# A hybrid mixer layer: order of the opening's weight casts, statistics and scale products

## The chip, the cores and the metric

The kernel runs on one core of a Trainium2 chip. The metric is the device time in microseconds (us) of one execution; lower is better. Engines are named as in the profile: PE is TensorE (matrix products and transposes), DVE is VectorE, ACT is ScalarE, POOL is GpSimd, SP is SyncE, whose queue issues nearly all DMAs.

## The reference

One layer with S = 2048 rows and D = 1024 columns, fp32. A modulated layer norm of x is projected, goes through a gated linear recurrence and an attention with forget gates, is projected back and normed again. Only the first lines matter for the opening:

```python
c_act = jax.nn.silu(c)
mod = c_act @ w_ada[l] + b_ada[l]
shift, scale, gate = jnp.split(mod, 3, axis=-1)
h = _layer_norm(x) * (1.0 + scale) + shift
proj = h @ w_in[l]
xr, zr, q, k, v, za, fl = jnp.split(proj, split_idx, axis=-1)
xc = _causal_depthwise_conv(xr, conv_w[l], conv_b[l])
y_r = _rms_norm(_rg_lru(xc, ...)) * silu(zr)
y_a = _rms_norm(_forgetting_attention(q, k, v, log_f)) * silu(za)
y = jnp.concatenate([y_r, y_a], axis=-1) @ w_out[l]
x = _layer_norm(ALPHA * x + gate * y) * ln_gain[l] + ln_bias[l]
```

## The kernel before

The rows are cut into four chunks (0 to 3) of 512 rows, each of four tiles of 128 rows. The columns D are cut into eight slabs k of 128. The opening, up to about 160 us, computes h transposed and the projection xr = h @ w_in[:, 0:512] of all four chunks; later stages project v, k, z, q and run the recurrence, the attention and the output.

**Norm of a tile** (`norm_tile`, L270, with `ln_stats`, L241). VectorE takes statistics (L244, L246) and adds eps (L248); GpSimd raises to the power -1/2 (rs, L250); VectorE makes nm = -mean x rs (L252); ScalarE applies both to one half of the tile or to both (L274), GpSimd to the other (L276).

**Column scale.** The factor 1 + scale of slab k needs a column block of w_ada (tile `wadab`, L640). TensorE multiplies the eight or four 128-row blocks of it with silu(c) (tile `psc`); from slab 2 on VectorE first folds the other half into a partial sum `sub` (L646, L648). VectorE writes the result into `Acol` (L653).

**First pass, chunks 0 and 1.** The products are fp32r with both operands in a high and a low half. For each slab, `load_w32` (L657) loads a row block of w_in (`wrow`), ScalarE casts it to the high half (L661) and GpSimd subtracts for the low half (L663). `make_h32` (L380) transposes the four normed tiles on TensorE (`ptr`, L387), ScalarE scales to the high half (L388), VectorE makes the low half (L389); for chunk 0 GpSimd joins both again (L378) into a spare part of XL. `xr32` (L610) does the twelve products of a slab: high by high, low weight by high, high weight by low. `xr32_out` copies the four sums to XL (L619). VectorE also takes column maxima of the weights (L167, `xam`) for the fp16 scales of the later chunks.

**Shift.** c_act @ w_ada for the shift (L745 to L753): slabs 0 to 4 are multiplied by ScalarE (L231) and added by GpSimd (L234), slabs 5 to 7 go through VectorE (L225, L227). VectorE adds the two parts (L811) ahead of the products `pada` (L824). `make_scale` (L337) turns the scale and the shift into Ash and Bcol.

**Second pass, chunks 2 and 3.** fp16 in two halves: `make_hk` (L394) transposes, ScalarE scales (hf, L400) and casts the high half (hT, L354), VectorE makes the low half (L355); `xr_k` does twelve products per slab. `finish_h` does the same for chunks 0 and 1 from the joined h. The maxima of the V weights (`amn`, L717 through L167) are taken in this pass.

**What sets the order.** The code is written in the order wanted; a scheduler with a timeline model then fixes each engine's queue. `tc.issue_after(ins)` holds back an instruction until the named one. Each engine runs its queue in order. SP's DMAs wait for their buffers and for the DMA issued eight places earlier. `spin` issues products of zeros on TensorE (22 + 12 + 8 of them in the opening). `QB` (L904) holds four query buffers of the attention; GpSimd clears one row of each (L1302).

Of the kernel before, what the change touches and what calls it, by code (L numbers as in the profile page):

```python
# [38 lines left out]
def hybrid_mixer(  # L39
# [201 lines left out]
    def ln_stats(halves, eps):  # L241
        st = sm([P, 2, 6], "bst")
        for g in range(2):
            nc.vector.bn_stats(st[:, g, :], halves[g])  # L244
# [3 lines left out]
        last["ve"] = nc.vector.tensor_scalar(ve, mv[:, 1:2], eps, None, ALU.add).ins  # L248
# [1 line left out]
        last["pow"] = nc.gpsimd.tensor_tensor(out=rs, in0=ve, in1=mhalf[:, 0:1], op=ALU.pow).ins  # L250
# [1 line left out]
        nc.vector.scalar_tensor_tensor(nm, mv[:, 0:1], -1.0, rs, ALU.mult, ALU.mult)  # L252
# [17 lines left out]
    def norm_tile(hv, n):  # L270
        rs, nm = ln_stats(hv, EPS)
        for g in range(2):
            if g < n:
                nc.scalar.activation(hv[g], hv[g], AF.Identity, scale=rs, bias=nm)  # L274
            else:
                last["pow"] = nc.gpsimd.tensor_scalar(hv[g], hv[g], rs, nm, ALU.mult, ALU.add).ins  # L276
# [103 lines left out]
    def make_h32(ci, k, xs):  # L380
        if k % 2 == 0:
            h32[ci, k // 2] = sb.tile([P, 2, 2, CH], F32R, name="h32", tag="H", bufs=8)
        t = h32[ci, k // 2]
        ps = bank("C", "ptr")
        ks = slice((k % 4) * P, (k % 4 + 1) * P)
        for i in range(4):
            nc.tensor.transpose(ps[:, i * P:(i + 1) * P], xs[i][k // 4][:, ks], ident)  # L387
# [269 lines left out]
    def load_w32(k):  # L657
# [3 lines left out]
        nc.scalar.copy(w[:, 0], raw)  # L661
# [138 lines left out]
    for k in range(KT + 2):  # L800
# [11 lines left out]
        if k > 1:  # L812
            xr32(pss, 1, k - 2)
        tick()
        if 3 <= k < 3 + 4:
            with tc.issue_after(last["lo"]), tc.issue_after(hi_act[1, k]):
                wu.append((split_T(xraw[k - 3], xrec[:, k - 3:k - 2]), xun[:, k - 3:k - 2]))
# [31 lines left out]
    new_h(2)  # L849
    new_h(0)  # L850
    for k in range(KT + 1):
        if k < KT:
            make_hk(2, k, xs2)
        if k > 0:
            xr_k(2, k - 1)
        if k < KT:
            with tc.issue_after(hi_act[2, k]),tc.issue_after(last["pow2"]):
                finish_h(0, k)
# [819 lines left out]
```

## Time and profile before

| | us |
|---|---|
| median of 3 runs (lowest, highest) | 1141.88 (1139.88, 1142.59) |
| profiled execution | 1142.41 |
| its span | 1140.7 |
| TensorE busy | 1091.2 (96%) |
| VectorE, ScalarE, GpSimd busy | 784.1, 708.3, 625.5 |
| first product of chunk 0, 1 and 2 in the opening | 20.44, 58.73, 93.79 |

In a timeline each line is a start, a duration, the engine, the line of the code, the operation, the tile written and the tiles read, the count of merged instructions and, in brackets, the idle time ahead with what ended it. An engine that waits costs time only if the end of the program hangs on it. The granted clock is the share of full speed that TensorE was given.

### The profile page before, as it was taken

How to read it: one execution, taken by the hardware profiler on the slowest of the kernel's cores; microseconds unless marked ns; L12 is line 12 of the kernel's file. 1: busy time of each engine (PE TensorE's matmuls, PEld its weight loads, DVE VectorE, ACT ScalarE, POOL GpSimd, SP SyncE). 2: the span in 40 equal slices, each digit the busy share in tenths (PEclk: the TensorE clock that was granted, in tenths of full speed). 3: DMA queues.
4: the chain of work that ended last, by engine and by line, in shares of the span. 5: the costliest groups of instructions: out<-in, count | busy, mean ns of one | idle time of the engine just before them, and what ended most of it. 6: DMA issues, size and time to landing. Idle time of an engine off the chain costs nothing.

```text
span 1140.7 us, 20267 instructions
## 1 busy us (share of the span) xinstructions
PE 1091.2 (96%) x7473; PEld 612.0 (54%) x7473; DVE 784.1 (69%) x1449; ACT 708.3 (62%) x1242; POOL 625.5 (55%) x655
## 2 busy tenths in 40 slices
PE   9999999999999999999889899999999999999887
PEld 6775545454544444444455455656555565566544
DVE  7877577776777963486655456678777877787546
ACT  3547746664767511544576677879777887787820
POOL 5725533454455300743267746878777687777731
PEclk8898999999999999999999999999999999999999
DMA  8862057210224711764454445124423134310111
GB/s 287 245 192 90 1 147 214 75 56 20 56 56 120 228 69 49 251 192 136 130 153 116 132 117 156 52 80 117 131 87 121 54 122 121 100 56 22 45 47 55
DMA packets 109415, 128.36 MB, mean 113 GB/s; under 512 B 10316, under 2 KB 79540, under 8 KB 109316
## 3 DMA queue, kind: packets, MB, share of 16 engines
q1 hardware_dynamic: 109088, 127.01, 36.6%
q8 instruction: 58, 0.95, 0.4%
q14 instruction: 41, 0.34, 0.1%
q10 hardware_dynamic: 228, 0.06, 0.0%
HBM read 97.57 MB, written 29.46 MB: 111 GB/s over the span
## 4 chain that ended last, share of the span: by engine, by line
PE 67%; DVE 10%; ACT 9%; issue 6%; POOL 4%; DMA 2%; SPq 1%; DVEq 0%; ACTq 0%; POOLq 0%
PE pj L93 26%; PE pout L93 13%; PE pst L93 8%; PE acc L93 6%; PE pmx L93 5%; PE pq L93 5%; ACT pf L1343 2%; DVE mc L1315 1%; PE pgate L93 1%; ACT ph L1345 1%; DVE wadab L648 1%; POOL XL L636 1%; POOL ph L1347 1%; DVE xres L1442 1%; ACT L515 1%
## 5 line engine op out<-in xcount | busy, mean ns | idle before, releaser
L1347 POOL TENSOR_TENSOR ph<-pf,ph 128x512 f16<-128x512 f32 (+2 forms) x240 | 266.6, 1125 | 110.9 <-ACT ph L1345 102.1
L93 PE MATMUL pj<-hT,wT 128*128 128x512 f16 x1440 | 321.8, 381 | 4.3 <-DVE sza L1192 2.6
L93 PEld LDWEIGHTS <-wT 128*128 128x128 f16 x1792 | 168.8, 98 | 199.9 <-issue 12.2
L1343 ACT ACTIVATE pf<-pst,bias 128x512 f32<-128x512 f32 (+1 forms) x320 | 196.7, 632 | 82.8 <-PE pst L93 80.5
L1315 DVE TENSOR_REDUCE mc<-pmx 128x1 f32<-128x512 f32 (+2 forms) x320 | 183.7, 602 | 87.5 <-PE pmx L93 83.5
L1345 ACT CAST ph<-pf 128x512 f16<-128x512 f32 (+1 forms) x320 | 173.1, 567 | 11.1 <-issue 3.8
L93 PE MATMUL acc<-V,ph 128*128 128x129 f16 (+1 forms) x2176 | 158.7, 209 | 10.5 <-POOL ph L1347 5.9
L93 PEld LDWEIGHTS <-ph 128*128 128x128 f16 x2176 | 126.5, 99 | 67.9 <-POOL ph L1347 10.6
L93 PE MATMUL pst<-qs,kk 128*128 128x512 f16 (+1 forms) x320 | 112.8, 354 | 2.7 <-ACT pf L1343 1.4
L93 PE MATMUL pst<-qb,kk 65*128 65x512 f16 (+1 forms) x320 | 111.0, 355 | 0.0
L93 PE MATMUL pmx<-kk,qb 67*128 67x512 f16 (+2 forms) x320 | 105.1, 357 | 5.3 <-DVE mc L1315 2.2
L93 PE MATMUL pout<-wo,yT 128*128 128x512 f16 (+1 forms) x396 | 97.3, 377 | 1.5 <-ACT yT L1423 1.5
L93 PE MATMUL pout<-wo,yr 128*128 128x512 f16 (+1 forms) x396 | 91.0, 373 | 0.1
L93 PE MATMUL pj<-wN,hT 128*128 128x512 f16 x384 | 89.4, 378 | 0.2 <-ACT XL L846 0.2
L1349 DVE TENSOR_TENSOR ph<-pf,ph 128x512 f16<-128x512 f32 (+1 forms) x80 | 58.9, 736 | 26.4 <-ACT ph L1345 22.4
L1246 POOL TENSOR_TENSOR XL<-XL,szr 128x512 f32<-128x512 f32 x16 | 24.8, 1551 | 89.8 <-ACT szr L1243 89.8
L93 PEld LDWEIGHTS <-kk 65*128 65x128 f16 (+1 forms) x640 | 54.5, 99 | 31.3 <-issue 7.6
L93 PEld LDWEIGHTS <-hT 128*128 128x128 f16 x640 | 44.6, 96 | 48.5 <-issue 3.3
L93 PE MATMUL pq<-hT,wT 128*128 128x512 f16 x288 | 67.9, 383 | 0.2 <-DVE qhl L916 0.2
L93 PEld LDWEIGHTS <-yT 128*128 128x128 f16 x396 | 37.5, 98 | 39.1 <-ACT yT L1423 1.7
L93 PEld LDWEIGHTS <-yr 128*128 128x128 f16 x396 | 37.4, 98 | 38.1 <-issue 0.7
L491 POOL TENSOR_TENSOR xl<-xc,xh 128x512 fp32r<-128x512 f32 x16 | 22.9, 1432 | 57.1 <-ACT xh L489 55.7
(311 smaller groups left out, 1784.9 us busy)
## 6 DMA issues: line engine op xcount, KB each, us to landing
wraw<-in_w_in_dram SPq DMA_DIRECT2D x40, 512.0 KB
woraw<-in_w_out_dram SPq DMA_DIRECT2D x16, 512.0 KB
xres<-in_x_dram SPq DMA_DIRECT2D x16, 512.0 KB
out_dram<-xres SPq DMA_DIRECT2D x15, 512.0 KB
xt<-in_x_dram SPq DMA_DIRECT2D x16, 256.0 KB
wadab<-in_w_ada_dram SPq DMA_DIRECT2D x8, 512.0 KB
xt<-in_x_dram SPq DMA_DIRECT2D x8, 512.0 KB
wsh<-in_w_ada_dram SPq DMA_DIRECT2D x16, 256.0 KB
```

Source lines behind the costliest of these rows:

```text
L93: m = nc.tensor.matmul(o, lhsT=l, rhs=r, start=st, stop=sp, skip_group_check=chk)
L491: nc.gpsimd.tensor_tensor(out=xl, in0=xc, in1=xh, op=ALU.subtract)
L515: nc.scalar.activation(a, r, AF.Exp, scale=L8n[:, j:j + 1])
L636: nc.gpsimd.tensor_scalar(XL[j][:, sl], XL[j][:, sl], 1.0, cs[j], ALU.mult, ALU.add)
L648: nc.vector.scalar_tensor_tensor(sub, blk[:, q - 1], cact[:, q - 1:q], sub, ALU.mult, ALU.add)
L1246: nc.gpsimd.tensor_tensor(out=XL[j][:, sl], in0=XL[j][:, sl], in1=sz, op=ALU.mult)
L1315: nc.vector.tensor_reduce(out=mc[:, i, b:b + 1], in_=ps[:, 0:w], axis=AX.X, op=ALU.max)
L1343: nc.scalar.activation(pf32[:, 0:w], ps[:, 0:w], AF.Exp, scale=DH ** -0.5, bias=bias[:, ci, h, kt:kt + 1])
L1345: nc.scalar.copy(ph[:, 0, 0:w], pf32[:, 0:w])
L1347: nc.gpsimd.tensor_tensor(out=ph[:, 1, 0:w], in0=pf32[:, 0:w], in1=ph[:, 0, 0:w], op=ALU.subtract)
L1349: nc.vector.tensor_tensor(ph[:, 1, 0:w], pf32[:, 0:w], ph[:, 0, 0:w], ALU.subtract)
L1442: nc.vector.scalar_tensor_tensor(xt[:, ns], xt[:, ns], rs, late["lnb"][:, ns], ALU.mult, ALU.add)
```

## The change

1. **nm on GpSimd.** `ln_stats` has a flag `pool`. With it VectorE writes ng = -mean and GpSimd multiplies nm = ng x rs. Chunks 0, 2 and 3 use it; chunk 1 keeps nm on VectorE.
2. **Pins.** The weight casts of the first pass are issued behind the last ScalarE norm of chunk 0. The norms of chunk 1 are issued behind the last low half of chunk 0 at their step, one step earlier than before (k = 4 to 7).
3. **First slabs.** The transposes of a slab come ahead of its scale products (`tr_h32`, `out_h32` split `make_h32`); the twelve products of slab 0 come ahead of the scale products of slab 1. The maxima of the weights run one slab later. The spins are 12 + 32 + 1.
4. **Shift.** The first part is written into two tiles `qa0`, `qa1` of their own; slab 5's product moves to ScalarE. `QB` now lies in `qa0`, `qa1`, so its clearing waits for the shift.
5. **Chunk 2.** x of chunk 2 is loaded at k = 2 instead of 3, its norms run at k = 3 to 6 instead of 4 to 7, and its first two slabs are transposed and scaled inside the loop of chunk 1. A doubled allocation of four banks goes.
6. **V weights.** Their loads are issued behind the last raw weight load.

The core of the diff:

```diff
-    def ln_stats(halves, eps):
+    def ln_stats(halves, eps, pool):
...
-        nc.vector.scalar_tensor_tensor(nm, mv[:, 0:1], -1.0, rs, ALU.mult, ALU.mult)
+        if pool:
+            ng = sm([P, 1], "ng")
+            nc.vector.tensor_scalar(ng, mv[:, 0:1], -1.0, None, ALU.mult)
+            last["pow"] = nc.gpsimd.tensor_tensor(out=nm, in0=ng, in1=rs, op=ALU.mult).ins
+        else:
+            nc.vector.scalar_tensor_tensor(nm, mv[:, 0:1], -1.0, rs, ALU.mult, ALU.mult)
...
-        nc.scalar.copy(w[:, 0], raw)
+        with tc.issue_after(last["nact0"]):
+            nc.scalar.copy(w[:, 0], raw)
...
-                    pa[g] = ada_add_pool(pa[g], w, k)
+                    if k == 0:
+                        pa[g] = con.tile([P, CH], F32, name=f"pa{g}", tag=f"qa{g}")
+                        nc.scalar.activation(pa[g], w, AF.Copy, scale=cact[:, 0:1])
+                    else:
+                        ada_add_pool(pa[g], w, k)
+            elif k == 5:
+                with tc.issue_after(after):
+                    nc.scalar.activation(w, w, AF.Copy, scale=cact[:, k:k + 1])
+                va[g] = w
...
-    spin(22)
+    spin(32)
...
     for k in range(KT + 1):
         if k < KT:
+            with tc.issue_after(last["pe"]):
+                ps = tr_h32(0, k, xs)
+            if k == 1:
+                spin(1)
+                x32_mm(0)
             with tc.issue_after(last["x0"]), tc.issue_after(last["pe"]):
                 scale_col(k)
                 load_w32(k)
-            with tc.issue_after(last["pe"]):
-                make_h32(0, k, xs)
-            if k < 2:
-                spin(4)
+            out_h32(0, k, ps)
...
-        if 5 <= k < 5 + 4:
-            norm_tile(xs1[k - 5], 1)
+        if 4 <= k < 8:
+            with tc.issue_after(last["lo"]):
+                norm_tile(xs1[k - 4], 1, False)
...
-    pss = [bank(t, "pj") for t in "BBAA"]
     pss = [bank(t, "pj") for t in "BBAA"]
...
+        if k == 2:
+            xs2 = load_x(2)
+        if 3 <= k < 7:
+            norm_tile(xs2[k - 3], 1)
...
+        if k >= KT:
+            if k == KT:
+                flush()
+                new_h(2)
+                new_h(0)
+            make_hk(2, k - KT, xs2)
...
-            vraw = vf_load()
+            with tc.issue_after(last["raw"]):
+                vraw = vf_load()
...
-    QB = [cst([67, CH], f"qb{i}", F16) for i in range(4)]
+    qa = [con.tile([67, 2, CH], F16, name=f"qa{g}", tag=f"qa{g}") for g in range(2)]
+    QB = [qa[i // 2][:, i % 2, :] for i in range(4)]
```

GpSimd's queue around the rs of chunk 1's fourth tile, before. `w` is the low half of a weight slab, `XL<-h` the join of a slab of chunk 0, `wsh` (later `pa`) an addition of the shift, `xt` the second half of a tile of chunk 1; the second `rs` is that of the fourth tile:

```order
L250 TENSOR_TENSOR rs<-ve,mhalf 128x1
L663 TENSOR_TENSOR w_570<-wrow,w_570 128x512
L378 TENSOR_TENSOR XL_125<-h_408 128x512
L276 TENSOR_SCALAR xt<-xt,rs,nm 128x512
L234 TENSOR_TENSOR wsh<-wsh 128x512
L250 TENSOR_TENSOR rs<-ve,mhalf 128x1
L234 TENSOR_TENSOR wsh<-wsh 128x512 x2
L378 TENSOR_TENSOR XL_125<-h_408 128x512
```

The same queue now; the last `rs` but one is that of chunk 1's fourth tile, the last that of chunk 2's first:

```order
L234 TENSOR_TENSOR pa_619<-pa_619,wsh 128x512
L382 TENSOR_TENSOR XL_126<-h_548 128x512
L234 TENSOR_TENSOR pa_623<-pa_623,wsh 128x512
L281 TENSOR_SCALAR xt<-xt,rs,nm 128x512
L250 TENSOR_TENSOR rs<-ve,mhalf 128x1
L281 TENSOR_SCALAR xt<-xt,rs,nm 128x512
L250 TENSOR_TENSOR rs<-ve,mhalf 128x1
```

The fourth rs moved from ahead of slab 5's join to behind slab 7's join and the last addition.

ScalarE's queue where chunk 0 ends (the copies of the four sums to XL) and chunk 1 begins (`h_686`, its first slabs), before:

```order
L274 ACTIVATE xt<-xt,nm,rs 128x512
L388 ACTIVATE h_520<-ptr,Acol 128x512
L231 ACTIVATE wsh<-wsh,cact 128x512 x2
L388 ACTIVATE h_520<-ptr,Acol 128x512
L231 ACTIVATE wsh<-wsh,cact 128x512 x2
L388 ACTIVATE h_686<-ptr,Acol 128x512
L619 COPY XL_123<-pj 128x512
```

The same place now, with `h_700` for chunk 1:

```order
L398 ACTIVATE h_548<-ptr,Acol 128x512
L231 ACTIVATE wsh<-wsh,cact 128x512 x2
L279 ACTIVATE xt<-xt,nm,rs 128x512
L629 COPY XL_123<-pj 128x512
L629 COPY XL_124<-pj 128x512
L629 COPY XL_125<-pj 128x512
L629 COPY XL_126<-pj 128x512
L279 ACTIVATE xt<-xt,nm,rs 128x512
L398 ACTIVATE h_700<-ptr,Acol 128x512
```

The norm of the fourth tile and the first scaling of chunk 1 moved behind the four copies.

VectorE's queue in chunk 2, before (`hT_1005`, `hT_1006` are slabs 0 to 3 and 4 to 7 of chunk 2, `hT_1007`, `hT_1008` those of chunk 0, `amn` the maxima of the V weights):

```order
L355 TENSOR_TENSOR hT_1006<-hf,hT_1006 128x512
L246 BN_AGGR mv<-bst 128x2
L355 TENSOR_TENSOR hT_1008<-XL_125,hT_1008 128x512
L248 TENSOR_SCALAR ve<-mv 128x1
L355 TENSOR_TENSOR hT_1006<-hf,hT_1006 128x512
L252 SCALAR_TENSOR_TENSOR nm<-mv,rs 128x1
L167 TENSOR_REDUCE amn<-wraw 128x1 x4
```

And now, with `hT_981`, `hT_982` for chunk 2 and `hT_983`, `hT_984` for chunk 0:

```order
L359 TENSOR_TENSOR hT_981<-hf,hT_981 128x512
L246 BN_AGGR mv<-bst 128x2
L248 TENSOR_SCALAR ve<-mv 128x1
L254 TENSOR_SCALAR ng<-mv 128x1
L167 TENSOR_REDUCE amn<-wraw 128x1 x4
L167 TENSOR_REDUCE amv<-wfraw 128x1
L359 TENSOR_TENSOR hT_983<-XL_124,hT_983 128x512
L359 TENSOR_TENSOR hT_982<-hf,hT_982 128x512
```

The four maxima moved from behind the low half of slab 5 of chunk 2 to ahead of that of slab 4.

More of the change, by code (lines that the diff above doesn't have):

```diff
@@ L268, in load_x, with norm_tile @@
         return xs
-    def norm_tile(hv, n):
-        rs, nm = ln_stats(hv, EPS)
+    def norm_tile(hv, n, pool=True):
+        rs, nm = ln_stats(hv, EPS, pool)
         for g in range(2):
             if g < n:
-                nc.scalar.activation(hv[g], hv[g], AF.Identity, scale=rs, bias=nm)
+                last["nact"] = nc.scalar.activation(hv[g], hv[g], AF.Identity, scale=rs, bias=nm).ins
             else:
@@ L310, in load_raw @@
         raw = r4([P, KT, P], "wraw")
-        nc.sync.dma_start(raw, w_in_v[:, :, col0:col0 + P])
+        last["raw"] = nc.sync.dma_start(raw, w_in_v[:, :, col0:col0 + P]).ins
         return raw
@@ L343, in make_scale @@
         nc.vector.scalar_tensor_tensor(bd, ma, 32.0, mb, ALU.mult, ALU.add)
-        yield
         bda = yield from all_max(bd, 1, 1)
@@ L380, in make_h32, with tr_h32, out_h32 @@
     def make_h32(ci, k, xs):
+        out_h32(ci, k, tr_h32(ci, k, xs))
+    def tr_h32(ci, k, xs):
+        ps = bank("C", "ptr")
+        ks = slice((k % 4) * P, (k % 4 + 1) * P)
+        for i in range(4):
+            last["pe"] = nc.tensor.transpose(ps[:, i * P:(i + 1) * P], xs[i][k // 4][:, ks], ident).ins
+        return ps
+    def out_h32(ci, k, ps):
         if k % 2 == 0:
@@ L383, in make_h32 @@
         t = h32[ci, k // 2]
[L384 to L387, printed above, removed]
         hi_act[ci, k] = nc.scalar.activation(t[:, k % 2, 0], ps, AF.Copy, scale=Acol[:, k:k + 1]).ins
@@ L742, in hybrid_mixer @@
     last["pow0"] = last["pow"]
+    last["nact0"] = last["nact"]
     va, pa = [None, None], [None, None]
@@ L755, in hybrid_mixer, with w_max, x32_mm @@
     xam = cst([P, 4, KT], "xam")
+    def w_max(k):
+        col_max(w32[k][:, 0].rearrange("p (j n) -> p j n", n=P), AX.X, xam[:, :, k])
     pss = [bank(t, "pj") for t in "AAAO"]
-    spin(22)
+    spin(32)
+    def x32_mm(k):
+        with tc.issue_after(last["pe"]):
+            xr32(pss, 0, k)
     for k in range(KT + 1):
         if k < KT:
+            with tc.issue_after(last["pe"]):
+                ps = tr_h32(0, k, xs)
+            if k == 1:
+                spin(1)
+                x32_mm(0)
             with tc.issue_after(last["x0"]), tc.issue_after(last["pe"]):
@@ L778, in hybrid_mixer @@
                 shift_slab(n, hi_act[0, n + KT - 5])
-        if k > 0:
-            with tc.issue_after(last["pe"]):
-                xr32(pss, 0, k - 1)
+        if k > 1:
+            x32_mm(k - 1)
             with tc.issue_after(last["lo"]):
-                col_max(w32[k - 1][:, 0].rearrange("p (j n) -> p j n", n=P), AX.X, xam[:, :, k - 1])
+                w_max(k - 2)
+    w_max(KT - 1)
     xr32_out(pss, 0)
-    pss = [bank(t, "pj") for t in "BBAA"]
     pss = [bank(t, "pj") for t in "BBAA"]
@@ L792, in xmax_fin @@
     def xmax_fin():
+        yield
         xcol = sm([P, 4], "xcol")
@@ L806, in hybrid_mixer @@
             xraw.append(load_raw(P * k))
+        if k == 2:
+            xs2 = load_x(2)
+        if 3 <= k < 7:
+            norm_tile(xs2[k - 3], 1)
         if k == 3:
-            xs2 = load_x(2)
             with tc.issue_after(last["lo"]):
@@ L811, in hybrid_mixer @@
                     nc.vector.tensor_tensor(va[g], va[g], pa[g], ALU.add)
[L812 to L817, printed above, removed]
         if k == 4:
@@ L827, in hybrid_mixer @@
             chains.append(make_scale())
-            tick()
-        if 4 <= k < 8:
-            norm_tile(xs2[k - 4], 1)
+        if k >= KT:
[4 more added lines that the diff above has]
+            make_hk(2, k - KT, xs2)
+        if k > 1:
+            xr32(pss, 1, k - 2)
+        tick()
+        if 3 <= k < 3 + 4:
+            with tc.issue_after(last["lo"]), tc.issue_after(hi_act[1, k]):
+                wu.append((split_T(xraw[k - 3], xrec[:, k - 3:k - 2]), xun[:, k - 3:k - 2]))
     last["pow2"] = last["pow"]
@@ L848, in hybrid_mixer @@
     pss = [bank(t, "pj") for t in "AOBB"]
[L849 to L858, printed above, removed]
+    for k in range(KT):
+        if k + 2 < KT:
+            make_hk(2, k + 2, xs2)
+        xr_k(2, k)
+        with tc.issue_after(hi_act[2, k]), tc.issue_after(last["pow2"]):
+            finish_h(0, k)
         if k == 4:
```

## The prediction

> **What bounds the kernel now.** I read the page first, then the busy time by stretches of 5 us over the first 200 us, then TensorE's timeline, then the timelines of the engines that feed it.
>
> ```profile
> span 1140.7 us, 20267 instructions
> PE 1091.2 (96%) x7473; PEld 612.0 (54%) x7473; DVE 784.1 (69%) x1449; ACT 708.3 (62%) x1242; POOL 625.5 (55%) x655
> ```
>
> TensorE is busy for 96% of the span, so time can be won only where it waits or runs at a low clock. The change touches the opening, up to the third chunk of rows; a shift there passes on to the end, because behind it TensorE is the busy engine. The profiled execution took 1142.41 us, 1.7 us beside its span; the median of the runs shown is 1141.88. I work from the profiled execution and take 0.5 us off at the end.
>
> The four columns that matter in the next view are the stretch, TensorE's busy time (the first after the comma) and, third from the end, the granted clock.
>
> ```profile
> 30.00:35.00 5.00, 5.00 (x32) 4.44 (x31) 4.29 (x9) 2.00 (x3) 3.46 (x4) 1.00 1.01 285
> 35.00:40.00 5.00, 3.52 (x19) 2.63 (x18) 4.96 (x12) 3.14 (x5) 4.02 (x5) 0.96 1.12 341
> 40.00:45.00 5.00, 4.65 (x14) 3.77 (x15) 4.96 (x10) 1.57 (x3) 3.67 (x4) 0.50 0.71 217
> 90.00:95.00 5.00, 3.63 (x13) 2.43 (x14) 2.75 (x7) 4.46 (x8) 4.57 (x7) 0.58 0.58 222
> 95.00:100.00 5.00, 5.00 (x22) 2.54 (x21) 4.83 (x12) 5.00 (x9) 2.11 (x3) 0.74 0.00 2
> ```
>
> TensorE idles 1.5 us at 35 to 40 and runs at half clock after it; the same happens around 90. The two stretches at 90 to 100 alone lose 5 x 0.42 + 5 x 0.26 = 3.4 us of clock.
>
> TensorE's timeline shows the projection of chunk 0 (slabs of 12 products), then of chunk 1 (from 58.73), then chunk 2 (from 93.79):
>
> ```profile
> 30.05 2.98 PE L93 MATMUL pj<-h,w 128*128 128x512 f32 x12
> ...
> 34.28 2.07 PE L93 MATMUL pj<-h,w 128*128 128x512 f32 x8
> ...
> 40.80 3.76 PE L93 MATMUL pj<-h,w 128*128 128x512 f32 x8
> ...
> 48.11 2.98 PE L93 MATMUL pj<-h,w 128*128 128x512 f32 x12
> ...
> 55.53 3.00 PE L93 MATMUL pj<-h,w 128*128 128x512 f32 x12
> ...
> 58.73 1.18 PE L93 MATMUL pj<-h,w 128*128 128x512 f32 x4
> ...
> 84.83 3.02 PE L93 MATMUL pj<-h,w 128*128 128x512 f32 x12
> ...
> 93.79 4.64 PE L93 MATMUL pj<-hT,wT 128*128 128x512 f16 x12
> ```
>
> An undisturbed slab takes 4.24 us from start to start (30.05 to 34.28, 48.11 to 52.35). Slab 3 takes 6.52 and slab 4 takes 7.31: the first pass loses 2.3 + 3.1 = 5.4 us there. What ends that wait stands on VectorE and GpSimd:
>
> ```profile
> 34.12 1.28 POOL L663 TENSOR_TENSOR w<-wrow,w 128x512 fp32r<-128x512 f32 x1
> 34.19 1.23 DVE L252 SCALAR_TENSOR_TENSOR nm<-mv,rs 128x1 f32<-128x1 f32 x1 [0.68 <-POOL rs L250]
> ...
> 35.34 1.27 DVE L244 BATCH_NORM_STATS2 bst<-xt 128x6 f32<-128x512 f32 x2
> ...
> 36.54 0.73 DVE L389 SCALAR_TENSOR_TENSOR h<-ptr,Acol,h 128x512 fp32r<-128x512 f32 x1
> ```
>
> The low half of slab 3 (36.54), which TensorE waits for, is queued behind the statistics of chunk 1: a wait of 0.68 for GpSimd, an nm of one column that takes 1.23 us because it lies beside GpSimd's operation, and 1.27 us of statistics.
>
> **The change part by part.** *First weights, spins, first slab.* The weight casts move behind chunk 0's last norm, the nm of chunk 0 to GpSimd.
>
> ```profile
> 14.69 0.16 DVE L252 SCALAR_TENSOR_TENSOR nm<-mv,rs 128x1 f32<-128x1 f32 x1 [0.66 <-POOL rs L250]
> 15.77 0.81 ACT L274 ACTIVATE xt<-xt,nm,rs 128x512 f32<-128x512 f32 x1
> 17.11 1.16 DVE L646 TENSOR_SCALAR wadab<-wadab,cact 128x128 f32<-128x128 f32 x1 [2.20 <-DMA wadab<-in_w_ada_dram]
> ```
>
> The last norm (15.77) can come 0.9 us earlier, since its nm ends at 14.85, and up to 2 us if VectorE's three waits of 0.66 for rs go. But the new order on VectorE puts the first column scale behind the partial sum of slab 2's block, which lands at 17.11. So the first product stays near its old start, and I take 0. The three extra spins cost nothing: they stand in that wait.
>
> ```profile
> 12.18 1.92 PE L93 MATMUL psc<-cact,wadab 128*128 128x1 f32 x16 [0.93 <-DMA wadab<-in_w_ada_dram]
> 20.44 4.07 PE L93 MATMUL pj<-h,w 128*128 128x512 f32 x12
> ```
>
> Slab 1's scale products, 1.92 us that used to lie in the wait before 20.44, now follow slab 0's 12 products: +1.9 on TensorE. Against it the 5.4 us of slabs 3 and 4 go, since the statistics are now issued behind the low half. TensorE could thus end the first pass 3.5 us earlier, at 55.0 instead of 55.53 + 3.00 = 58.53.
>
> *What is late next: GpSimd.* The same pinning puts the rs of chunk 1's fourth tile at the end of GpSimd's queue. In before it is at 47.23; behind it there are still seven additions of the shift and three joins.
>
> ```profile
> 47.23 0.66 POOL L250 TENSOR_TENSOR rs<-ve,mhalf 128x1 f32<-128x1 f32 x1 [0.29 <-DVE ve L248]
> ...
> 60.03 1.48 POOL L234 TENSOR_TENSOR wsh<-wsh 128x512 f32<-128x512 f32 x1
> ```
>
> The groups of GpSimd between 14 and 64 us (count, busy, mean ns):
>
> ```profile
> L378 POOL TENSOR_TENSOR XL<-h 128x512 f32<-128x512 f32 x8 | 10.5, 1316 | 2.5 <-DVE h L389 2.5
> L234 POOL TENSOR_TENSOR wsh<-wsh 128x512 f32<-128x512 f32 x8 | 10.4, 1315 | 0.7 <-ACT wsh L231 0.7
> L663 POOL TENSOR_TENSOR w<-wrow,w 128x512 fp32r<-128x512 f32 x8 | 10.3, 1295 | 2.0 <-ACT w L661 2.0
> L276 POOL TENSOR_SCALAR xt<-xt,rs,nm 128x512 f32<-128x512 f32 x5 | 3.9, 771 | 1.0 <-DVE nm L252 0.4 <-DVE Acol L653 0.3
> L250 POOL TENSOR_TENSOR rs<-ve,mhalf 128x1 f32<-128x1 f32 x5 | 3.0, 593 | 5.8 <-DVE ve L248 5.8
> ```
>
> In the new order GpSimd must, from the join of slab 3 up to the fourth rs, do 14 operations of about 1.31 us (five joins, one weight, eight additions), four rs of 0.59 and three xt of 0.77: 18.3 + 2.4 + 2.3 = 23.0 us. That join waits for slab 3's low half, which on VectorE now stands behind slab 6's block of w_ada. In the DMA queue that block comes after slab 5's weight row:
>
> ```profile
> 27.81 0.35 SPq L659 DMA_DIRECT2D wrow<-in_w_in_dram  x1
> ```
>
> From this row to slab 6's block the new queue issues four pieces of 256 KB and three of 512 KB, 2.6 MB in all. At the 285 to 341 GB/s of the stretches above that is 8 to 9 us. The issue at 27.81 can come 1.5 us earlier, since a 512 KB tile of x that stood ahead of it now stands behind it, so the block lands between 34.3 and 36.8; I take 36.0. VectorE has three operations on it ahead of the low half:
>
> ```profile
> L648 DVE SCALAR_TENSOR_TENSOR wadab<-wadab,cact 128x128 f32<-128x128 f32 x18 | 12.4, 690 | 0.3
> ```
>
> 3 x 0.69 + 0.73 = 2.8, so the join can begin at 38.8, and 23.0 more make 61.8 for the fourth rs.
>
> Behind it stand nm, one norm, four transposes and one scaling before chunk 1's first product:
>
> ```profile
> 47.72 0.64 PE L387 MATMUL ptr<-ident,xt 128*128 128x128 f32 x4
> ...
> 49.22 0.82 ACT L274 ACTIVATE xt<-xt,nm,rs 128x512 f32<-128x512 f32 x1 [1.24 <-DVE nm L252]
> 49.94 0.67 ACT L388 ACTIVATE h<-ptr,Acol 128x512 fp32r<-128x512 f32 x1
> 58.06 2.04 ACT L619 COPY XL<-pj 128x512 f32<-128x512 f32 x4
> ```
>
> 0.16 + 0.82 + 0.64 + 0.67 is 2.3 us, so 64.1 instead of 58.73: **+5.4**. The lower bound is GpSimd without a pause after slab 5's weight, which cannot be cast before 28: 28 + 4 x 1.31 + 23.0 + 2.3 = 58.5, so 0. The upper bound: VectorE's sums each wait for a GpSimd operation, as the nm at 34.19 did for 1.2 us; three such waits make it 3.6 later, +9.0. I take +5.4, the sum of the rows. Even without GpSimd the fourth norm stands behind the four copies (2.04) on ScalarE, so the first product comes no earlier than about 3.5 us after the first pass ends.
>
> *The clock.* TensorE then idles for more than 4 us before 64.1, longer than the 1.5 us that halved the clock at 40. The new drop costs between 1.0 and 3.4 us (the loss at 90 to 100); part lies in the wait: **+2.0**. The Trainium skill, "TensorE: Matmul & The Clock Gate", Part 1, says the throttle returns after one idle window of about 3.4 us. By that rule a 4 us gap may hold no full window, and this term would be 0; the rows at 35 to 45 show a drop after 1.5 us of idle time in pieces, so the trace decides for the drop.
>
> *Chunk 1 and the entry of chunk 2.* Six single transposes of chunk 2 (0.64 / 4 each) move into chunk 1: **+0.9**. The memset of QB (four small ones) and the nm on GpSimd lie in its free time there (GpSimd is done with the first pass's work by then). The k = 5 product of the shift goes from VectorE to ScalarE, beside other work. Chunk 2's statistics come earlier, and the wait after 84.83 + 3.02 = 87.85 shrinks: it was 5.94 us to 93.79. Now the copies, two hf and one cast are in the way:
>
> ```profile
> 91.20 1.45 ACT L400 ACTIVATE hf<-ptr,Bcol,Ash 128x512 f32<-128x512 f32 x2 [0.54 <-PE ptr L398]
> ...
> 92.54 0.61 ACT L354 CAST hT<-hf 128x512 f16<-128x512 f32 x1
> ...
> 105.97 4.59 DVE L167 TENSOR_REDUCE amn<-wraw 128x1 f32<-128x1024 f32 x4
> ```
>
> Copies that start 0.65 before the end (2.04), 1.45 and 0.61 leave 3.5: -2.4. The half clock there may go: 0 to -2.0. Against both, the four maxima of the V weights (4.59) now stand ahead of slab 4's low half on VectorE instead of behind slab 5's, up to +2.8. Together **-2.0**, bounds -4.4 and +0.4. The aliasing of QB, the single allocation of banks and the small reorderings behind 500 us I cost at 0: the buffers there are free long before; uncovered, each would cost about one operation of 1.3 us.
>
> Sum: 5.4 + 2.0 + 0.9 - 2.0 = +6.3. From 1142.4 that is 1148.7, against the median **1148.2**.
>
> **The rivals.** *GpSimd keeps pace* (its bound, 0; clock +1.0; +0.9; entry -4.4): -2.5, so 1139.4, no difference that can be told (a measurement tells 0.3%, 3.4 us, from no change). For it: GpSimd sits idle for 12.0 us in the five groups above; against it: slab 6's block cannot land before 34.3, and 2.8 + 23.0 us follow it. Chance 0.19. That the casts' pin does nothing, since casts wait for their rows anyway, leads to the same place.
>
> *Faster:* the first pass's 3.5 us come through. The place is the start of chunk 1: it decides if the fourth rs is done by 56, so that only the copies are in the way and chunk 1 starts at 58.5. Then 0 there, +0.9, -4.4 and up to -2 from the earlier first norm: -3.5 to -5.5, so 1137.4. For it: the losses of slabs 3 and 4 are in the rows. Against it: 23 us of GpSimd's work stand ahead. Chance 0.15.
>
> *No drop of the clock* (the page's rule above): the drop's term falls away, +4.3, so 1146.2, still slower; within the forecast, with 0.1 of its chance.
>
> **How the numbers follow.** The forecast case has 0.66, its own range 1139.4 (all low bounds: 0 + 1.0 + 0.9 - 4.4) to 1155.6 (9.0 + 3.4 + 0.9 + 0.4); 0.08 of it lies within 3.4 us of before. So faster 0.15, same 0.19 + 0.08 = 0.27, slower 0.58. The range leaves out about 0.1 on each side: 1138.0 to 1153.0.
>
> **What would show it.** In the new trace: TensorE's slabs 3 and 4 at 4.2 to 5 us; GpSimd without a pause from about 39 to 62, its fourth rs of chunk 1 at 60 to 63; a gap of 3 us or more on TensorE before chunk 1's first product and half clock after it; 3.5 to 4 us from chunk 1's last product to chunk 2's first. It is wrong if chunk 1 starts before 60, or if the gap there is shorter than 2 us.

## The result, and the profile after

The changed kernel takes 1146.86 us (median, 1142.85 to 1154.89); the kernel before, measured beside it, 1140.22 (1136.64 to 1146.85). The ratio is 1.0054, with a 95% interval of 1.004 to 1.0068: slower by 0.54%, which is 6.2 us by the ratio and 6.6 by the medians. The profiled execution took 1146.86 us:

```profile
span 1144.9 us, 20306 instructions
PE 1090.0 (95%) x7476; PEld 608.9 (53%) x7476; DVE 781.4 (68%) x1447; ACT 708.7 (62%) x1244; POOL 628.3 (55%) x667
```

TensorE's work is the same; it waits more, or at other places. Its timeline, with chunk 0 from 20.16, chunk 1 from 68.23 and chunk 2 from 100.34:

```profile
20.16 5.43 PE L93 MATMUL pj<-h,w 128*128 128x512 f32 x12 [3.45 <-ACT h L398]
...
28.64 4.58 PE L93 MATMUL pj<-h,w 128*128 128x512 f32 x12
...
46.75 5.47 PE L93 MATMUL pj<-h,w 128*128 128x512 f32 x12
...
61.08 3.01 PE L93 MATMUL pj<-h,w 128*128 128x512 f32 x12
...
67.12 0.44 PE L391 MATMUL ptr<-ident,xt 128*128 128x128 f32 x2 [2.59 <-ACT xt L279]
68.23 2.12 PE L93 MATMUL pj<-h,w 128*128 128x512 f32 x8 [0.67 <-ACT h L398]
...
95.87 1.17 PE L93 MATMUL pj<-h,w 128*128 128x512 f32 x4
...
100.34 4.44 PE L93 MATMUL pj<-hT,wT 128*128 128x512 f16 x12
```

The first pass ends at 61.08 + 3.01 = 64.09 (before 58.53): +5.56. The wait behind it, up to chunk 1, is 4.14 (before 58.73 - 58.53 = 0.20): +3.94. From chunk 1's first product to chunk 2's it takes 32.11 (before 93.79 - 58.73 = 35.06): -2.95. Together +6.55 at chunk 2, about what the medians show at the end.

The same stretches by granted clock (third column from the end):

```profile
20.00:25.00 5.00, 4.84 (x11) 3.80 (x12) 4.64 (x7) 1.35 (x3) 3.78 (x4) 0.50 1.07 379
25.00:30.00 5.00, 5.00 (x36) 4.61 (x35) 2.28 (x6) 0.69 (x1) 0.45 (x1) 0.84 0.46 140
...
45.00:50.00 5.00, 5.00 (x22) 4.32 (x21) 4.40 (x11) 2.18 (x4) 5.00 (x5) 0.59 0.52 142
...
65.00:70.00 5.00, 2.21 (x10) 1.68 (x11) 2.05 (x5) 3.80 (x7) 1.79 (x3) 1.00 0.28 85
```

The half clock lies in slabs 0 and 1 and in slab 4, and not where chunk 1 begins. The last column, the rate of the DMAs in GB/s, falls to 140 between 25 and 30 us. VectorE, ahead of slabs 3 and 4, waits for blocks of w_ada:

```profile
36.10 0.29 DVE L656 TENSOR_SCALAR wadab<-wadab,cact 128x128 f32<-128x128 f32 x1 [3.01 <-DMA wadab<-in_w_ada_dram]
...
37.46 0.15 DVE L663 SCALAR_TENSOR_TENSOR Acol<-psc,c_ada 128x1 f32<-128x1 f32 x1
38.80 0.28 DVE L656 TENSOR_SCALAR wadab<-wadab,cact 128x128 f32<-128x128 f32 x1 [1.18 <-DMA wadab<-in_w_ada_dram]
...
39.77 0.75 DVE L399 SCALAR_TENSOR_TENSOR h<-ptr,Acol,h 128x512 fp32r<-128x512 f32 x1
...
42.63 0.63 DVE L656 TENSOR_SCALAR wadab<-wadab,cact 128x128 f32<-128x128 f32 x1 [0.60 <-DMA wadab<-in_w_ada_dram]
43.19 0.14 DVE L663 SCALAR_TENSOR_TENSOR Acol<-psc,c_ada 128x1 f32<-128x1 f32 x1
```

These rows (L656) begin the folds of the blocks of slabs 5, 6 and 7. In VectorE's queue the scale of slab 3 (37.46) stands behind the first fold, its low half (39.77) behind the second, the scale of slab 4 (43.19) behind the third. So does the copy of the small vectors (44.55), which ended a wait of 1.67 us on TensorE at 44.80. On GpSimd, the join of slab 3, the two pauses behind it and the fourth rs of chunk 1:

```profile
40.59 1.29 POOL L382 TENSOR_TENSOR XL<-h 128x512 f32<-128x512 f32 x1 [4.40 <-DVE h L399]
...
44.74 2.63 POOL L234 TENSOR_TENSOR pa<-pa,wsh 128x512 f32<-128x512 f32 x2 [1.56 <-ACT wsh L231]
...
55.99 1.27 POOL L234 TENSOR_TENSOR pa<-pa,wsh 128x512 f32<-128x512 f32 x1 [1.89 <-ACT wsh L231]
...
65.48 0.55 POOL L250 TENSOR_TENSOR rs<-ve,mhalf 128x1 f32<-128x1 f32 x1
```

And on ScalarE the four copies and the fourth norm:

```profile
63.45 2.05 ACT L629 COPY XL<-pj 128x512 f32<-128x512 f32 x4 [0.31 <-PE pj L93]
66.26 0.81 ACT L279 ACTIVATE xt<-xt,nm,rs 128x512 f32<-128x512 f32 x1 [0.76 <-DVE nm L257]
```

The copies end at 65.50 and the rs starts at 65.48: a tie, with the rs last by 0.76 us.

### The profile page after: what moved, and what is told of

It reads as the page before. It is cut to its first block, busy times and chain, and to the rows that moved or that the text cites. A ratio compares the mean times of both kernels' runs of the same rounds, so it can differ in the third digit from the quotient of the medians.

```text
span 1144.9 us, 20306 instructions
## 1 busy us (share of the span) xinstructions
PE 1090.0 (95%) x7476; PEld 608.9 (53%) x7476; DVE 781.4 (68%) x1447; ACT 708.7 (62%) x1244; POOL 628.3 (55%) x667
## 4 chain that ended last, share of the span: by engine, by line
PE 69%; DVE 10%; ACT 8%; issue 5%; POOL 4%; DMA 3%; SPq 1%; DVEq 0%; ACTq 0%; POOLq 0%
PE pj L93 28%; PE pout L93 13%; PE pst L93 8%; PE acc L93 6%; PE pq L93 5%; PE pmx L93 4%; DVE mc L1351 2%; ACT pf L1379 1%; PE pgate L93 1%; DMA wadab<-in_w_ada_dram 1%; DVE xres L1478 1%; POOL ph L1383 1%; POOL XL L646 1%; ACT ph L1381 1%; ACT L525 1%
## 5 line engine op out<-in xcount | busy, mean ns | idle before, releaser
L93 PE MATMUL pst<-qa,kk 65*128 65x512 f16 (+1 forms) x320 | 109.6, 351 | 0.0
L93 PE MATMUL pmx<-kk,qa 67*128 67x512 f16 (+2 forms) x320 | 102.4, 351 | 4.2 <-DVE mc L1351 1.7
L93 PE MATMUL pj<-h,w 128*128 128x512 f32 x192 | 56.0, 443 | 4.1 <-ACT h L398 4.1
```

Of the source, the lines that this page charges most:

```text
L93: m = nc.tensor.matmul(o, lhsT=l, rhs=r, start=st, stop=sp, skip_group_check=chk)
```

## The experiments

All are edits of the changed kernel, but for e8, an edit of the kernel before, and the two repeats e11 and e12. "Last pf" is the start of the last product of the forget gates (tile pf), a mark behind the opening and the V projection. The places are those of one profiled execution, the median is of 6 to 20 executions (of one for e11 and e12), and the ratio is to the kernel before, run beside it. The runs were taken in groups (after; e1 to e4; e5 to e8; e9 to e12), between which the median of the kernel before moved by 1.2 us.

| run | pass ends | chunk 1 | chunk 2 | last pf | median us | ratio (95%) |
|---|---|---|---|---|---|---|
| before | 58.53 | 58.73 | 93.79 | 249.9 | 1140.2 to 1141.4 | 1 |
| after | 64.09 | 68.23 | 100.34 | 256.8 | 1146.86 | 1.0054 (1.004 to 1.0068) |
| e1 spins | 60.16 | 67.37 | 102.34 | 257.9 | 1148.82 | 1.0073 (1.0049 to 1.0097) |
| e2 statistics | 64.03 | 64.22 | 96.73 | 252.7 | 1141.25 | 1.0004 (0.9983 to 1.0025) |
| e3 first slabs | 54.93 | 63.87 | 98.01 | 255.0 | 1146.74 | 1.0054 (1.0036 to 1.0073) |
| e4 vectors | 59.17 | 65.14 | 99.39 | 256.7 | 1147.90 | 1.007 (1.0045 to 1.0095) |
| e5 relief | 62.43 | 65.86 | 99.59 | 256.7 | 1147.38 | 1.0063 (1.0042 to 1.0084) |
| e6 = e3 + e5 | 55.66 | 61.14 | 95.41 | 250.7 | 1140.50 | 1.0 (0.9985 to 1.0016) |
| e7 = e2 + e3 | 59.72 | 59.91 | 92.31 | 249.0 | 1137.39 | 0.9966 (0.9947 to 0.9985) |
| e8 chunk 2 alone | 58.63 | 58.82 | 92.39 | 249.7 | 1139.11 | 0.9986 (0.997 to 1.0002) |
| e9 = e6 + copies | 55.26 | 59.06 | 91.86 | 246.7 | 1137.05 | 0.9962 (0.9944 to 0.998) |
| e10 = e7 + copies | 60.23 | 60.42 | 91.51 | 246.3 | 1139.31 | 0.998 (0.9964 to 0.9995) |
| e11 after again | 66.57 | 70.62 | 102.73 | 259.2 | 1148.34 | none |
| e12 before again | 57.44 | 57.64 | 94.27 | 250.9 | 1143.83 | none |

**e2, the statistics' pin undone.**

```diff
-        if 4 <= k < 8:
-            with tc.issue_after(last["lo"]):
-                norm_tile(xs1[k - 4], 1, False)
+        if 5 <= k < 9:
+            norm_tile(xs1[k - 5], 1, False)
```

> Edit of the changed kernel: the norms of chunk 1 run one step later and unpinned, as before the change. Theory of GpSimd's queue (the prediction's step): the gap of 4.1 us between the first pass's end (64.09) and chunk 1's first product (68.23) goes to about 0.2, since the fourth rs leaves the end of the queue and the fourth norm gets ahead of the four copies; gain about 4 us. Rival, the statistics come back ahead of slab 3's and 4's low halves: these slabs, 7.91 and 7.08 us now, grow by 1 to 3 us and the gain is 0 to 2. If the late blocks of w_ada set slabs 3 and 4, they do not grow.

The gap went to 0.19, and the time back to that of before. TensorE where the passes meet:

```profile
61.01 3.02 PE L93 MATMUL pj<-h,w 128*128 128x512 f32 x12
...
64.22 1.18 PE L93 MATMUL pj<-h,w 128*128 128x512 f32 x4
```

Slabs 3 and 4 did not grow (5.98 and 5.89 us from start to start); the statistics now cost 3.35 us ahead of slab 1, and the pass ends where it did. Taking away the pin, and with it the earlier step, takes the loss away; the two were not undone one by one.

**e1, the clock in slabs 0 and 1.**

```diff
-                spin(1)
+                spin(13)
```

> Edit of the changed kernel: 13 products of zeros instead of 1 ahead of slab 0, so that TensorE does not idle for 3.45 us before 20.16. Theory of the clock: that idle time halves the clock in slabs 0 and 1, which took 5.43 and 4.58 us for 12 products where an undisturbed slab takes 3.00; with the spins they take 3.0 to 3.5, the first pass ends 2.5 to 4 us earlier (60 to 61.6 instead of 64.09) and the run gains about 3 us. Theory of GpSimd's queue: the first product of chunk 1 waits for the fourth rs, which hangs on GpSimd's own 23 us of work, so the pass may end earlier but chunk 1 still starts at 67.5 to 68.5 and the run gains under 1 us.

```profile
20.61 3.07 PE L93 MATMUL pj<-h,w 128*128 128x512 f32 x12 [0.83 <-ACT h L398]
...
63.48 0.69 PE L391 MATMUL ptr<-ident,xt 128*128 128x128 f32 x2 [3.10 <-ACT xt L279]
...
67.37 3.78 PE L93 MATMUL pj<-h,w 128*128 128x512 f32 x8 [0.56 <-ACT h L398]
```

Slab 0 runs at full clock (3.07 instead of 5.43) and the pass ends 3.9 us earlier, where the theory of the clock put it, but for another reason. Slab 1 still has the half clock (4.27), and slab 2 starts only 0.9 us earlier (33.62 instead of 34.53). The rest comes from slabs 3 and 4, which take 4.77 and 5.40 us instead of 7.91 and 7.08. Their blocks are no earlier: those of slabs 5, 6 and 7 are issued at 29.81, 30.30 and 35.76 (in the changed kernel at 29.52, 30.01 and 35.31), and VectorE still waits for two of them. What differs is VectorE's queue:

```profile
33.79 0.16 DVE L663 SCALAR_TENSOR_TENSOR Acol<-psc,c_ada 128x1 f32<-128x1 f32 x1 [1.00 <-PE psc L93]
36.59 0.29 DVE L656 TENSOR_SCALAR wadab<-wadab,cact 128x128 f32<-128x128 f32 x1 [2.64 <-DMA wadab<-in_w_ada_dram]
...
37.18 0.74 DVE L399 SCALAR_TENSOR_TENSOR h<-ptr,Acol,h 128x512 fp32r<-128x512 f32 x1
...
39.36 0.28 DVE L656 TENSOR_SCALAR wadab<-wadab,cact 128x128 f32<-128x128 f32 x1
...
40.85 0.15 DVE L663 SCALAR_TENSOR_TENSOR Acol<-psc,c_ada 128x1 f32<-128x1 f32 x1
...
42.52 1.26 DVE L656 TENSOR_SCALAR wadab<-wadab,cact 128x128 f32<-128x128 f32 x1 [0.81 <-DMA wadab<-in_w_ada_dram]
```

Here the scheduler put slab 3's scale (33.79) ahead of the fold of slab 5's block, its low half (37.18) ahead of that of slab 6's, and slab 4's scale (40.85) ahead of that of slab 7's; in the changed kernel each stands behind that fold. So the late blocks cost their stall through this order, and hardly without it.

Chunk 1 starts only 0.9 earlier; the longer wait ahead of it ends with the half clock (3.78 us for eight products that took 2.12), and the time does not fall. A faster first pass is worth nothing while the fourth norm comes late.

**e3, the first slabs' order undone.**

```diff
-    spin(32)
+    spin(22)
...
-            with tc.issue_after(last["pe"]):
-                ps = tr_h32(0, k, xs)
-            if k == 1:
-                spin(1)
-                x32_mm(0)
...
-            out_h32(0, k, ps)
+            with tc.issue_after(last["pe"]):
+                make_h32(0, k, xs)
+            if k < 2:
+                spin(4)
...
-        if k > 1:
+        if k > 0:
             x32_mm(k - 1)
```

> Edit of the changed kernel: slab 0's twelve products go back behind slab 1's scale products, with 22 + 4 + 4 spins as before the change; everything else stays changed. Theory of the first slabs: slab 0 and slab 1 together took 14.37 us from start to start against 9.61 before; 4.8 us come back (1.9 of scale products, 2.9 of clock), the first pass ends near 59.5 and the run gains 4 to 5 us. Theory of GpSimd's queue: chunk 1 starts no earlier than 66.5, and the gain is under 1.5 us.

Each theory is right in one half. The pass ends 9.2 us earlier, not 4.6: slabs 3 and 4 take 5.40 and 4.56 us instead of 7.91 and 7.08. Chunk 1 starts 4.4 us earlier, so GpSimd's end was not fixed: its chain begins with slab 3's low half, which comes earlier too (32.42), and the fourth rs (60.98) here waited last for VectorE (0.84 us). The gain, none, is as the theory of GpSimd's queue has it: the median is that of the changed kernel.

```profile
51.78 3.15 PE L93 MATMUL pj<-h,w 128*128 128x512 f32 x12
...
60.17 0.69 PE L391 MATMUL ptr<-ident,xt 128*128 128x128 f32 x2 [4.92 <-ACT xt L279]
...
63.87 3.78 PE L93 MATMUL pj<-h,w 128*128 128x512 f32 x8 [0.56 <-ACT h L398]
```

Two things differ where slabs 3 and 4 recover, of which e1 had only the first. VectorE's queue again has slab 3's scale (30.16) and low half (32.42) ahead of the fold of slab 5's block (33.68). And SyncE's queue issues slab 7's block earlier. Here the block of slab 5 is issued at 28.74 and those of slabs 6 and 7 from 30.81:

```profile
28.74 0.40 SPq L650 DMA_DIRECT2D wadab<-in_w_ada_dram  x1
...
30.81 1.42 SPq L650 DMA_DIRECT2D wadab<-in_w_ada_dram  x2
```

In the changed kernel slab 7's block goes out only at 35.31, behind three more pieces of the shift:

```profile
29.52 1.31 SPq L650 DMA_DIRECT2D wadab<-in_w_ada_dram  x2
33.36 1.85 SPq L760 DMA_DIRECT2D wsh<-in_w_ada_dram  x3
35.31 0.38 SPq L650 DMA_DIRECT2D wadab<-in_w_ada_dram  x1
```

The code that was written behind the transposes, `scale_col`, also issues the loads: the new order of the first slabs moved the load of the last slab back by 4.0 us (31.29 to 35.31).

**e4, the vector loads out of SyncE's queue** (to ScalarE's queue at the start):

```diff
+    vcol = load_cols([(conv_w, 16), (conv_b, 4), (b_gate_a, 4), (b_gate_x, 4), (lru_lambda, 4),
+                      (norm_lru, 4), (norm_attn, 4)], "vec", nc.scalar)
...
-            vcol = load_cols([(conv_w, 16), (conv_b, 4), (b_gate_a, 4), (b_gate_x, 4), (lru_lambda, 4),
-                              (norm_lru, 4), (norm_attn, 4)], "vec", nc.sync)
```

> Edit of the changed kernel: the seven small vector loads (r_vec) go from SyncE's queue, where they stand between 20.2 and 27.2 us ahead of slab 5's weight row, to ScalarE's queue at the start. Theory of late blocks: slabs 3 and 4 wait for VectorE, which waits for the blocks of w_ada of slabs 5, 6 and 7 (landed at 36.10, 38.80 and 42.6); with the queue free from 20 the blocks land 3 to 6 us earlier, slabs 3 and 4 take 4.3 to 5 us instead of 7.91 and 7.08, and the pass ends 4 to 6 us earlier. If the transfer of chunk 1's x (2 MB) and the buffers set these landings, they move by under 1 us and nothing is gained. Theory of GpSimd's queue: even with the blocks earlier the fourth rs stays within 2 us of 65.5.

Slabs 3 and 4 take 4.28 and 4.34 us, and the pass ends at 59.17, 4.9 earlier, as the theory of late blocks forecast. But the blocks of slabs 5, 6 and 7 go out at 27.91, 29.19 and 35.07, only 1.6, 0.8 and 0.2 us earlier:

```profile
35.07 0.38 SPq L655 DMA_DIRECT2D wadab<-in_w_ada_dram  x1
```

VectorE's queue has the order of e1 and e3 once more: slab 3's scale (35.02) and low half (35.94) ahead of the fold of slab 5's block (37.20), slab 4's low half (41.37) ahead of that of slab 7's (45.30). The copy of the vectors is out of the way too (14.24). So this run does not show that earlier blocks end the stall; it shows the order again. No run has early blocks in the changed kernel's order.

The fourth rs moved by 3.2 us (to 62.25), more than the other theory allowed. The time did not fall: chunk 1's first eight products again took 3.78 us.

**e5, GpSimd's queue relieved.**

```diff
-        if ci == 0:
+        if ci == 0 and k < 3:
             join(0, k, h0f(k))
...
-                norm_tile(xs1[k - 4], 1, False)
+                norm_tile(xs1[k - 4], 2, False)
...
+    with tc.issue_after(last["pow"]):
+        for k in range(3, KT):
+            join(0, k, h0f(k))
```

> Edit of the changed kernel that touches GpSimd's queue alone: the joins of slabs 3 to 7 of chunk 0 (5 x 1.3 us) go behind chunk 1's fourth norm, and ScalarE does both halves of chunk 1's norms (3 x 0.77 us less ahead of the fourth rs). Theory of GpSimd's queue: the fourth rs comes 4 to 9 us earlier than 65.48, the fourth norm no longer waits for it, and chunk 1's first product follows the pass's end by 0.2 to 3.5 us instead of 4.1 (3.5 if the norm still stands behind the four copies on ScalarE); gain 1 to 4 us. Theory that the statistics' pin on VectorE (behind slab 7's low half) or the copies on ScalarE set chunk 1's start: the rs comes under 3 us earlier, and nothing is gained.

```profile
61.05 0.55 POOL L250 TENSOR_TENSOR rs<-ve,mhalf 128x1 f32<-128x1 f32 x1
```

```profile
61.77 1.56 ACT L629 COPY XL<-pj 128x512 f32<-128x512 f32 x3 [1.68 <-PE pj L93]
63.21 1.53 ACT L279 ACTIVATE xt<-xt,nm,rs 128x512 f32<-128x512 f32 x2
```

The rs comes 4.4 us earlier and chunk 1 2.4 earlier, 3.4 behind the pass's end: now three copies and a norm of both halves on ScalarE come last. Nothing was gained, though a gain of 1 to 4 us was expected. The half clock came again (2.86 us for the eight products), and the last pf product is at the changed kernel's place. GpSimd's queue alone is not the cause.

**e6, both edits of e3 and e5.**

> The same relief of GpSimd's queue, on the run in which slab 0's products went back behind slab 1's scale products. There the pass ended at 54.93 but chunk 1 started at 63.87, with the fourth rs at 60.98 and half clock in chunk 1's first slabs (0.50 and 0.68). Theory of GpSimd's queue: the fourth rs comes at 53 to 55, chunk 1 starts at 57 to 59, the wait is too short for the half clock, and the run gains 4 to 7 us against that one (1140 to 1143, near or below before). If the copies or the pin on VectorE set the start, chunk 1 stays at 62 or later and the time at 1145 to 1148.

```profile
59.38 0.69 PE L391 MATMUL ptr<-ident,xt 128*128 128x128 f32 x2 [3.06 <-ACT xt L279]
61.14 3.78 PE L93 MATMUL pj<-h,w 128*128 128x512 f32 x8 [1.07 <-ACT h L398]
```

Chunk 1 starts at 61.14, between the two theories, and the time falls by 6.2 us to 1140.5. Here, where the pass ends early, the queue does bind. The fourth rs, at 56.69 where 53 to 55 was expected, waited for VectorE's statistics (54.90), which stand behind slab 7's low half (52.61), two maxima and an nm.

**e7, both edits of e2 and e3.**

> Both undone in the changed kernel: chunk 1's norms unpinned as before, and slab 0's products behind slab 1's scale products as before. What stays of the change: nm on GpSimd, the casts' pin, the shift, the early norms of chunk 2. If these two parts are the whole loss, chunk 1 starts at 58.5 to 60 as before the change, and the entry of chunk 2 (3.3 us instead of 5.94) brings 2 to 3 us: 1137 to 1139. If another part (the weight maxima one slab later, the shift on ScalarE, the loads of the V weights) costs something too, the time is 1141 or more.

As expected: chunk 1 at 59.91, the time 1137.39. The two parts together are the whole loss and more; what is left of the change is a gain of 0.34% (0.15 to 0.53) over the kernel before. What the part of e3 adds to that of e2 is smaller than the noise can bear: the intervals of e2 and e7 just overlap.

**e8, the kernel before with the early chunk 2 alone.**

```diff
-        if k == 3:
+        if k == 2:
             xs2 = load_x(2)
+        if 3 <= k < 7:
+            norm_tile(xs2[k - 3], 1)
...
+        if k >= KT:
+            if k == KT:
+                flush()
+                new_h(2)
+                new_h(0)
+            make_hk(2, k - KT, xs2)
```

> The kernel before with one part of the change alone: x of chunk 2 loaded one step earlier, its norms one step earlier, its first two slabs transposed and scaled inside chunk 1's loop. By the prediction's entry term (-2.0, and +0.9 for the transposes inside chunk 1) the wait between chunk 1's last and chunk 2's first product goes from 5.94 to about 3.5 and the run gains 1 to 3 us: 1137.5 to 1139.5. Rival: the clock there halves as before and the four copies still stand in the way, so under 1 us is gained.

The wait ahead of chunk 2 is 2.60 us (92.39 less 89.79) instead of 5.94. The median falls by 2.3 us as expected, but the interval of the ratio just reaches 1, so a gain is likely and not shown.

**e9, e6 with two of the four copies on VectorE.**

```diff
-            nc.scalar.copy(XL[j][:, 3 + ci * CH:3 + (ci + 1) * CH], pss[j])
+            (nc.vector.tensor_copy if j % 2 else nc.scalar.copy)(XL[j][:, 3 + ci * CH:3 + (ci + 1) * CH], pss[j])
...
-                norm_tile(xs1[k - 4], 2, False)
+                norm_tile(xs1[k - 4], 2 if k < 7 else 1, False)
```

> The run with GpSimd relieved and slab 0's products back behind slab 1's scale products (median 1140.5; pass ends at 55.66, chunk 1 starts at 61.14, chunk 2 at 95.41), with two of the four copies of a chunk's sums on VectorE instead of ScalarE and one half of the fourth norm back on GpSimd. Theory that ScalarE's queue is next (three copies, 1.53 us, and a norm of both halves, 1.52, stand ahead of chunk 1's first scaling): chunk 1 starts 1 to 2 us earlier, chunk 2's entry (3.3 us) is 1 us shorter, and the time falls by 2 to 3 us to about 1138. Rival, the pin behind slab 7's low half: the fourth rs stays at 56.7, chunk 1 starts within 0.7 us of 61.14, and only chunk 2's entry gains: 1139 to 1140.5.

Chunk 1 starts 2.1 us earlier (59.06), chunk 2's entry shrinks from 3.29 to 2.33, and the time falls by 3.45 to 1137.05, faster than the kernel before by 0.38% (0.2 to 0.56). The fourth rs stays where it was (56.31), so what stood behind it, ScalarE's queue, was next.

**e10, e7 with the same split of the copies.**

> The fastest run so far (statistics unpinned, slab 0's products behind slab 1's scale products; median 1137.39), with two of the four copies of a chunk's sums on VectorE. If the copies on ScalarE are what is left of the wait ahead of chunk 2 (hf, 1.90 us of wait, behind 2.03 us of copies), its first product follows chunk 1's last by about 2.3 us instead of 3.3 to 3.6, a gain of 1 us: 1136 to 1137. If VectorE's queue there (statistics of chunk 3, low halves) delays the copies, nothing is gained or up to 1 us is lost.

The entry shrinks as expected (2.32 instead of 3.56), the last pf product comes 2.7 us earlier, and yet the median is 1.9 higher. The intervals of e7 and e10 overlap: inconclusive.

**e11 and e12, the changed kernel and the kernel before once more.**

> The changed kernel once more, for the scatter of one profile: if the opening repeats, the first pass ends within 1 us of 64.09, chunk 1 starts within 1 us of 68.23 and the V projection (first wN product) within 1.5 us of 153.98; if the half clock falls differently from run to run, these move by 2 to 4 us, and single traces cannot bear differences of that size.

> The kernel before once more, for the same purpose: chunk 1 within 1 us of 58.73, chunk 2 within 1.5 us of 93.79, the first wN product within 1.5 us of 147.17 if the opening repeats; otherwise 2 to 4 us away.

```profile
70.62 2.11 PE L93 MATMUL pj<-h,w 128*128 128x512 f32 x8 [0.67 <-ACT h L398]
```

The changed kernel's pass ended at 66.57, 2.5 us later than in the first profile, with the stall of slabs 3 and 4 again (9.05 and 7.13 us); the wait of 4.05 ahead of chunk 1 and that of 3.30 ahead of chunk 2 are the same to 0.1 us. In the kernel before, chunk 1 started at 57.64 (1.1 earlier) and chunk 2 at 94.27. The opening of the changed kernel thus did not repeat within 1 us, the first case of its expectation, and moved by 2 to 3 us, the second. Waits at a fixed place repeat; how long a pass takes moves by 2.5 us, so no verdict here rests on one pass's end alone.

## Why the prediction was right or wrong

The forecast was 1148.2 (+6.3) and the measurement 1146.86 (+6.6). The direction came from the right step, but that the sum agrees to 0.3 us is luck: chunk 1's start was 4.1 us later than its term, the clock's term of 2.0 fell away, and the way from chunk 1 to chunk 2 was 1.9 us shorter than its terms.

- **First slab, 0.** Right: 20.16 against 20.44. But "the three extra spins cost nothing" overlooked what the moved scale products leave behind: TensorE waits 3.45 us in one piece, and slabs 0 and 1 take 5.43 and 4.58 us instead of 4.07 and 3.01. That is 2.9 us that no term had; with the 12 spins of e1 it is 0.3.
- **Slab 1's scale products, +1.9.** Seen: psc x16 takes 1.84 behind slab 0.
- **Slabs 3 and 4, -5.4.** Wrong. The statistics left, but the two slabs take 14.99 us instead of 13.83. The step that failed is that the wait was taken to vanish with the statistics. In its term for GpSimd the prediction itself put slab 3's low half behind slab 6's block, at 38.1 instead of 36.54 before; in its term for TensorE it left that out. The trace shows the scales and the low half behind the folds of three blocks, which landed at 36.10, 38.80 and 42.63. Two landings were off as well: slab 6's block was put at 36.0, but the 2.6 MB from the row at 27.18 took 11.6 us, 226 GB/s and not 285 to 341; and the sum did not have slab 7's block. In e1, with blocks as late but the other order on VectorE, the stall is gone. Of the 14.99 us, 2.5 are the half clock in slab 4 (5.47 instead of 3.0). So the pass ended at 64.09 instead of 55.0.
- **GpSimd, rs at 61.8.** The fourth rs ended at 66.03. The join began at 40.59 instead of 38.8, and from there it took 25.4 us instead of 23.0: 22.0 of work, where 23.0 were counted, and 3.4 in two pauses for ScalarE, where the prediction had none. The 2.3 us behind the rs are 2.2. Chunk 1's start was thus +9.5 instead of +5.4, 0.5 beyond the upper bound of +9.0. This is the prediction's main step, and it carried the sign: e2 shows that the early, pinned norms hold the loss. But the queue was not the only thing in the way, as the prediction had it: e5 relieved it and gained nothing, since behind the pin the copies and the norm follow at once.
- **Clock, +2.0 behind that wait.** Wrong place: the granted clock is 1.00 around that wait, in both profiles of the changed kernel, so there the rival without a drop (1146.2) is what happened. By the prediction's own places the wait would have been 9 us (55.0 to 64.1), not just "more than 4"; it was 4.1, since the pass ended late. In e1, e3, e4 and e6 the drop came, with eight products at 3.78 us. The cost of the half clock fell into slabs 0, 1 and 4 instead.
- **Chunk 1 and the entry of chunk 2, +0.9 and -2.0.** The wait there is 3.30 (100.34 less 97.04) where 3.5 was said. From chunk 1 to chunk 2 it is -2.95 in all, not -1.1: the transposes cost nothing that can be seen (chunk 1 takes 28.8 us; before 29.1, and 30.7 in its second profile). The half clock stayed (4.44 for the first twelve products, before 4.64), and no loss to the maxima of the V weights shows: chunks 2 and 3 take 53.64 us up to the V projection, before 53.38.

Of the signs that it named, the wait before chunk 1 came (2.59 and 0.67 us of idle time), and chunk 2's entry was near; slabs 3 and 4 at 4.2 to 5 us, GpSimd without a pause, the fourth rs at 60 to 63 and the half clock behind the wait did not come. The kernel that it described is nearly e3, without the reordered first slabs: there the pass ends at 54.93 (forecast 55.0), the fourth rs at 61.53 (61.8), chunk 1 starts at 63.87 (64.1), and the half clock follows. Part of that is chance too, since e3's fourth rs waited last for VectorE.

Open: behind 150 us the kernels run the same work, yet against the kernel before the last pf product and the medians move by amounts up to 3 us apart (e2 +2.8 and +0.9, e3 +5.1 and +6.4, e7 -0.9 and -4.0). The granted clock is part of it. In the 22 executions of the kernel before beside e9 to e12 it varies by itself: the shortest took 1133.85 us at a mean clock of 0.986, the longest 1145.65 at 0.980. One profile for each run cannot settle the rest.

## What to carry to other kernels

Moving a step's code moves its loads too: follow each DMA that it issues to its new place in the queue, and ask what stands behind its landing in the queue of the engine that waits for it. An order that one term of a sum relies on must go into every term. Work that is pinned behind the last step of a pass makes a serial chain at the seam of two passes, and to take one link out of it (GpSimd's queue here) gains nothing while the next link, another engine's copies, ends at the same time. Look at the seam with all its engines, and undo each part of a change alone before keeping the sum.
